# Pacing the first weights by the landing of the x tiles, throwaway matmuls in TensorE's waits, and a last tile in two halves, in an eight-core decoder step

## The chip, the cores and the metric

The kernel runs on all 8 cores of one Trainium2 chip, two dies of four cores. Each core works on its own prompt and its own four samples, and the cores exchange nothing. The metric is the device time of the slowest core in microseconds (us), as a median of several executions.

Such a program has a second, slower state: in some executions one die runs at a lower granted clock (0.812 on four cores in a run of the kernel before that took 2145.57 us). All comparisons here are between fast runs. Where a sentence speaks of "span" it means the time from the first to the last instruction of one core in the trace; the device time is 1.5 to 2.5 us longer. In the views, PE is TensorE's matmuls and PEld its weight loads, DVE is VectorE, ACT ScalarE, POOL GpSimd and SP SyncE; a "q" after a name marks the engine's sequencer, which issues transfers. L80 is the one line of a helper through which every recorded operation goes, so operations are told apart by their tiles.

## The reference

One layer of a hybrid decoder: half an FFN, a mixer of three branches, half an FFN, a final norm. Cut to what matters here:

```python
def rmsnorm(x, g):
    xf = x.astype(jnp.float32)
    y = xf * lax.rsqrt(jnp.mean(xf * xf, axis=-1, keepdims=True) + EPS)
    return (y * g.astype(jnp.float32)).astype(x.dtype)

def half_ffn(x, g, w_gate, w_up, w_down):
    h = rmsnorm(x, g)
    return (jax.nn.silu(h @ w_gate) * (h @ w_up)) @ w_down

# per layer, for prompt (2048 rows a core) and samples (4 rows a core) alike:
x = x + 0.5 * half_ffn(x, *ffn1)
x = x + merge_branches(attention, hgrn2, memory)       # the mixer, cut here
x = x + 0.5 * half_ffn(x, *ffn2)
# at the end:
y = rmsnorm(x, g_final)
```

The model width is 1024 and the FFN's 2816 = 22 x 128. The change touches the first norm and the first gate and up products (the head), and the last down product and the final norm (the tail).

## The kernel before

A core's 2052 rows are six tiles of 352, 336, 336, 352, 336 and 340 columns; a tile of x is `[128, 8, n]` in f32, 1.38 to 1.44 MB. The first half of the program works on tiles 0 to 2, which this document calls the first, second and third tile.

The kernel's Python does not write instructions in the order of the source. It records operations, and a small list scheduler ("the planner") gives every engine one fixed order, using its own table of durations and landing times. On the chip each engine runs that order strictly: an operation whose data is ready still stands behind the one planned before it. PSUM tiles come from pools that hand out banks in order:

```python
# planner
DMA_RATE = {SP: 130.0, POOL: 190.0, ACT: 100.0}          # bytes per ns that it assumes per queue
# ...
def grab(o, t):
    for v in o["allocs"]:
        pl = v.pool
        while pl.first < len(pl.tiles) and pl.tiles[pl.first].unit is not None:
            pl.first += 1                                   # first tile without a bank
        if v.seq > pl.first + pl.ahead:
            return None, pl                                 # too far ahead of it: parked
        # ... take a free bank
# ...
psA = P.pool(bu[0:5], True, 3)                              # gate, up and down products: 5 banks, 3 ahead
```

The head:

```python
def sq(k, c, late=1000.0, pair=True):                       # with pair=False, as in the head
    # ...
    actf(b.t[:, 0:n], xv(k, c), AF.Square, [dx[k][c]], [b.d])
    mm(p.t[:, 0:n], ones_n, b.t[:, 0:n], c == 0, c == 7, [b.d, dc], [p.d], late=late)

def rstd(k):                                                # Ln, then Exp(-0.5 * ..), on ACT
    # ...
    lnexp(r.t[:, 0:n], p.t[:, 0:n], -0.5, [p.d], [r.d])
    return r

def to_h(k, r, g):                                          # the normalized tile, on DVE
    for c in range(8):
        stt(DVE, hT[:, c, t0:t0 + n], xv(k, c), g[:, c:c + 1], r.t[:, 0:n], ALU.mult, ALU.mult, ...)

def gate_up(half, w, hook=None):
    for j in range(NJ):                                     # 22 weights, each 1 MB read as f32, 512 KB as bf16
        b = load_w(..., 2048, first_w[min(j, 5)] if hook else ())   # POOL's queue; waits for these x parts
        for k in HT[half]:                                  # three tiles
            pg, pu = P.tile(psA), P.tile(psA)
            for p, a in ((pg, 0), (pu, 1)):
                for c in range(8):
                    mm(p.t[:, 0:n], wv[:, a, c, :], hT[:, c, t0:t0 + n], c == 0, c == 7, [b.d, dh[k][c]], [p.d])
            actf(s.t[:, 0:n], pg.t[:, 0:n], AF.Silu, [pg.d], [s.d])
            tt(DVE, act[:, j, o:o + n], pu.t[:, 0:n], s.t[:, 0:n], ALU.mult, ...)

first_w = [dx[0][0:4], dx[0], dx[1][0:4], dx[1], dx[2][0:4], dx[2]]
# ...
load_x(0, xt, 4, queues=(SP, ACT))
# ... constants ...
P.dma(ACT, lambda e: e.dma_start(out=vec[:, 0:52], in_=vecs), writes=[dc])
for k in range(3):
    if k:
        load_x(k, xt, 2, after=dx[k - 1][0:5] if k == 1 else dx[k - 1][0:4])
    for c in range(8):
        sq(k, c, 0.0, False)
    to_h(k, rstd(k), gf1)
```

The tail is the general `down`, which does the last two 128-row output chunks tile by tile, and `fin`, which squares, sums, scales and stores a whole tile:

```python
def down(half, w, done):
    def one(k, dp, bs):
        p = P.tile(psA)
        for j in range(NJ):
            mm(p.t[:, 0:n], ..., act[:, j, o:o + n], j == 0, j == NJ - 1, ...)
        stt(DVE, xv(k, dp), p.t[:, 0:n], 0.5, xv(k, dp), ALU.mult, ALU.add, ...)   # residual
        sq(k, dp)
    # ... chunks 0 to 5 for all three tiles, then
    for k in HT[half]:
        for dp, bs in last:                                 # chunks 6 and 7
            one(k, dp, bs)
        done(k)                                             # fin(k): Ln, Exp, eight scalings, four stores
```

The softmax here doesn't subtract the row's maximum and nothing guards it: scores larger than these inputs give would overflow.

## Time and profile before

| what | value | view |
|---|---|---|
| device time, median of 3 runs | 1804.74 us (1804.11 to 1805.31) | times |
| TensorE (PE) busy | 1738.2 us, 96% of the span | the page, part 1 |
| share of PE in the chain that ended last | 90% | the page, part 4 |
| PE idle between 160 and 1730 us | 15.1 us | the waits view |
| gate and up matmuls begun by 50 us | 74 | windows |
| last down matmul to the end of the span | 18.3 us | timeline |

The page of the kernel before has the span, the busy time of each engine (with its share and its number of instructions), and the chain of work that ended last, by engine:

```profile
span 1802.6 us, 33178 instructions; the slowest of 8 cores (1797.5 to 1802.6 us)
...
PE 1738.2 (96%) x12105; PEld 1109.0 (62%) x12171; DVE 674.7 (37%) x1391; ACT 730.4 (41%) x1266; POOL 405.2 (22%) x543
...
PE 90%; DVE 3%; ACT 3%; issue 2%; DMA 1%; POOL 1%; DVEq 0%; ACTq 0%; SPq 0%; POOLq 0%
```

TensorE is nearly always busy, so time can be won only where it is not: at the start and at the end. The windows view of core 2, restricted to the instructions that read or write the normalized tile `hT`, counts gate and up matmuls. Its columns are the stretch and its length, the busy time (and number) of PE, of weight loads and of DVE, the granted TensorE clock, the DMA engines' share and GB/s:

```profile
20.00:30.00 10.00, 3.91 (x16) 1.87 (x16) 4.06 (x8) 1.00 0.99 263
30.00:40.00 10.00, 7.15 (x32) 3.58 (x32) 3.92 (x8) 0.83 1.04 196
40.00:50.00 10.00, 6.42 (x26) 3.48 (x27) 3.92 (x8) 0.66 0.64 143
0.00:50.00 50.00, 17.48 (x74) 8.93 (x75) 11.90 (x24) 0.90 0.83 182
```

At the warm spacing of 0.143 us, 74 matmuls are 10.6 us of work in 50 us, so 39.4 us are lost in the head. The clock falls to 0.83 and 0.66 as well: after the pauses TensorE is cold, that is, it runs at a lower granted clock.

The timeline of core 2 shows why. Its columns are the start, the duration of the group, engine, line, operation, output and input, shape and number; in brackets the idle time of the engine before it and what ended it.

```profile
2.19 0.34 ACTq L80 DMA_DIRECT2D vec<-vecs  x1
...
9.54 3.94 ACT L80 ACTIVATE br<-XA,vec 128x352 bf16<-128x352 f32 x8 [5.98 <-DMA vec<-vecs]
...
14.17 0.56 ACT L80 ACTIVATE fr<-hb,vec 128x352 f32<-128x352 f32 x1 [0.69 <-PE hb L80]
...
21.17 0.57 ACT L80 ACTIVATE br<-XA,vec 128x336 bf16<-128x336 f32 x1 [6.44 <-DMA XA<-xt]
...
21.65 0.57 ACT L80 ACTIVATE fr<-fr,vec 128x352 f32<-128x352 f32 x1
...
22.32 4.06 DVE L80 SCALAR_TENSOR_TENSOR hT<-XA,vec,fr 128x352 bf16<-128x352 f32 x8 [20.59 <-ACT fr L80]
...
23.06 0.79 PE L80 MATMUL ps<-hT,wp 128*128 128x352 bf16 x2
...
42.87 3.92 DVE L80 SCALAR_TENSOR_TENSOR hT<-XA,vec,fr 128x336 bf16<-128x336 f32 x8 [1.93 <-ACT fr L80]
```

The squares of the first tile wait until 9.54 us for the small vector of constants, not for x, though the last part of x had landed only at 9.2. The Ln of the first tile runs at 14.17, but its Exp only at 21.65: it stands in ACT's fixed order behind one square of the second tile (21.17), which waits 6.44 us for its load.

The timeline of core 2 at the end:

```profile
1781.70 2.61 PE L80 MATMUL nd<-actb,wp 128*128 128x340 bf16 x17
...
1783.52 3.91 DVE L80 SCALAR_TENSOR_TENSOR XB<-XB,vec,fr 128x336 f32<-128x336 f32 x8
...
1787.35 0.50 DVE L80 SCALAR_TENSOR_TENSOR XB<-nd,XB 128x340 f32<-128x340 f32 x1
...
1791.56 4.53 DVE L80 SCALAR_TENSOR_TENSOR XB<-XB,vec,fr 128x340 f32<-128x340 f32 x5 [3.71 <-ACT fr L80]
...
1797.36 0.35 ACTq L80 DMA_DIRECT2D yt<-XB  x1
```

The last down matmul ends at 1784.31. Then DVE still scales the tile before (1783.52 for 3.91 us) ahead of the last residual addition.

### The profile page before, as it was taken

The page shows a single profiled execution, that of the slowest core. Times are in us where ns is not written, and L with a number is a line of the kernel's source. Part 1 is how long each engine was busy: PE and PEld are TensorE (multiplying, and loading weights), DVE is VectorE, ACT ScalarE, POOL GpSimd, SP SyncE. Part 2 cuts the span into 40 slices and gives each one's busy share as a digit, 9 for nine tenths or more (in the row PEclk, how much of TensorE's full clock was granted, in tenths as well). Part 3 has the DMA queues.
Part 4 walks back from the last instruction along what each step waited for, and adds up shares of the span by engine and source line. Part 5 has one row for each costly group of instructions (what it writes and reads, how often), then busy time and mean ns, then how long its engine had stood idle before and what let it go on. Part 6 is the DMA issues. An engine that isn't in the chain of part 4 may idle for free.

```text
span 1802.6 us, 33178 instructions; the slowest of 8 cores (1797.5 to 1802.6 us)
## 1 busy us (share of the span) xinstructions
PE 1738.2 (96%) x12105; PEld 1109.0 (62%) x12171; DVE 674.7 (37%) x1391; ACT 730.4 (41%) x1266; POOL 405.2 (22%) x543
## 2 busy tenths in 40 slices
PE   4999999999999999999999999999999999999996
PEld 1666666666655545555556566666666666666663
DVE  2223314222142435756576533543452221422213
ACT  5334414222145566758776633433342221322212
POOL 1112221001244051433431122322220002100021
PEclk9999999999999999999999999999999999999998
DMA  8486459656688554654547745596875447899562
GB/s 196 80 167 127 70 102 197 123 122 127 120 211 199 142 120 77 122 98 93 96 100 152 170 80 88 106 193 130 164 147 87 69 104 145 163 192 171 104 141 96
DMA packets 89391, 234.00 MB, mean 130 GB/s; under 512 B 32912, under 2 KB 40336, under 8 KB 86416
## 3 DMA queue, kind: packets, MB, share of 16 engines
q0 software_dynamic: 40608, 127.03, 44.6%
q1 hardware_dynamic: 46224, 59.26, 10.4%
q10 hardware_dynamic: 2400, 45.57, 8.7%
q8 instruction: 102, 1.67, 0.4%
q14 instruction: 57, 0.47, 0.1%
HBM read 321.27 MB, written 80.51 MB: 223 GB/s over the span
## 4 chain that ended last, share of the span: by engine, by line
PE 90%; DVE 3%; ACT 3%; issue 2%; DMA 1%; POOL 1%; DVEq 0%; ACTq 0%; SPq 0%; POOLq 0%
PE ps L80 49%; PE nd L80 33%; PE hb L80 8%; DVE XB L80 1%; ACT fr L80 1%; DMA XA<-xt 1%; DVE hT L80 1%; DVE br L80 1%; ACT br L80 0%; ACT L80 0%; ACT XA L80 0%; DVE fr L80 0%; POOL XA L80 0%; DVE XA L80 0%; POOL fr L80 0%
## 5 line engine op out<-in xcount | busy, mean ns | idle before, releaser
L80 PE MATMUL ps<-hT,wp 128*128 128x336 bf16 (+4 forms) x3839 | 637.2, 312 | 5.7 <-DVE hT L80 3.8
L80 PEld LDWEIGHTS ps<-hT,wp 128*128 128x128 bf16 x3856 | 365.6, 98 | 208.3 <-issue 6.4
L80 PE MATMUL nd<-hT,wp 128*128 128x336 bf16 (+4 forms) x2547 | 434.5, 312 | 1.4 <-ACT fr L80 0.2
L80 PEld LDWEIGHTS nd<-hT,wp 128*128 128x128 bf16 x2560 | 243.3, 98 | 134.7 <-issue 2.0
L80 ACT ACTIVATE fr<-ps,vec 128x336 f32<-128x336 f32 (+3 forms) x269 | 150.1, 560 | 343.8 <-PE ps L80 343.4
L80 PE MATMUL ps<-actb,wp 128*128 128x336 bf16 (+2 forms) x1612 | 253.8, 308 | 0.3 <-DVE XB L80 0.3
L80 PEld LDWEIGHTS ps<-actb,wp 128*128 128x128 bf16 x1612 | 157.3, 98 | 76.7 <-issue 0.6
L80 ACT ACTIVATE fr<-nd,vec 128x336 f32<-128x336 f32 (+3 forms) x185 | 103.4, 560 | 235.5 <-PE nd L80 235.2
L80 DVE TENSOR_TENSOR actb<-ps,fr 128x336 bf16<-128x336 f32 (+2 forms) x160 | 81.9, 514 | 266.2 <-PE ps L80 260.9
L80 PE MATMUL nd<-actb,wp 128*128 128x336 bf16 (+2 forms) x1076 | 173.0, 308 | 0.7 <-ACT fr L80 0.7
L80 POOL TENSOR_TENSOR fr<-fr 128x512 f32<-128x512 f32 (+3 forms) x96 | 108.0, 1132 | 161.0 <-DVE fr L80 140.2
L80 POOL DMA_DIRECT2D wp<-wgu x88 | 47.4, 538 | 400.3 <-PE ps L80 229.9
L80 PEld LDWEIGHTS nd<-actb,wp 128*128 128x128 bf16 x1076 | 105.0, 98 | 52.3 <-issue 1.0
L80 POOL TENSOR_TENSOR br<-fr 128x336 bf16<-128x336 f32 (+2 forms) x84 | 77.3, 923 | 181.2 <-ACT fr L80 181.0
L80 DVE TENSOR_TENSOR actb<-nd,fr 128x336 bf16<-128x336 f32 (+2 forms) x104 | 53.2, 513 | 173.2 <-PE nd L80 167.2
L80 ACT ACTIVATE fr<-XB,vec 128x352 f32<-128x352 f32 (+2 forms) x96 | 53.9, 577 | 138.5 <-DVE XB L80 138.5
L80 PE MATMUL hb<-hT,wp 128*128 128x512 bf16 (+1 forms) x514 | 95.2, 312 | 1.0 <-ACT fr L80 0.2
L80 ACT ACTIVATE fr<-XA,vec 128x336 f32<-128x336 f32 (+1 forms) x72 | 40.9, 578 | 130.2 <-DVE XA L80 130.2
L80 POOL DMA_DIRECT2D wp<-wd x64 | 34.8, 544 | 249.6 <-PE ps L80 128.5
L80 PE MATMUL hb<-br,cb 128*128 128x336 bf16 (+7 forms) x188 | 48.5, 300 | 28.9 <-ACT br L80 22.9
L80 ACT ACTIVATE fr<-fr,vec 128x512 f32<-128x512 f32 (+3 forms) x105 | 72.6, 700 | 5.0
L80 DVE SCALAR_TENSOR_TENSOR fr<-fr,ps 128x336 f32<-128x336 f32 (+2 forms) x85 | 43.2, 510 | 77.6 <-ACT fr L80 77.6
(244 smaller groups left out, 1630.9 us busy)
## 6 DMA issues: line engine op xcount, KB each, us to landing
wp<-wgu POOLq DMA_DIRECT2D x88, 512.0 KB, 8.9
wp<-wd POOLq DMA_DIRECT2D x64, 352.0 KB, 5.8
wp<-w_gb POOLq DMA_DIRECT2D x48, 384.0 KB, 8.8
wp<-w_hqf POOLq DMA_DIRECT2D x16, 512.0 KB, 8.3
vd<-br SPq DMA_DIRECT2D x48, 128.0 KB, 4.0
XA<-vd SPq DMA_DIRECT2D x12, 512.0 KB, 5.7
wp<-w_qk POOLq DMA_DIRECT2D x12, 512.0 KB, 7.6
pv<-fr SPq DMA_DIRECT2D x21, 256.0 KB, 6.4
```

Source lines behind the costliest of these rows:

```text
L80: return f(*[g(x) for x in a], **{n: g(x) for n, x in k.items()})
```

## The change

In the head, all x tiles are queued at once in four parts each, the constants first; the first weight goes at once, later ones when given parts of x have landed; squares go to ACT or DVE; and the planner puts throwaway matmuls wherever it plans a wait of TensorE in the first 60 us. It also assumes 150 bytes per ns on every queue in the first 30 us. In the tail, the last tile is done as two halves of 168 and 172 columns, each with its own sum, scaling and store; outputs are written into a contiguous buffer; Exp also writes its result to PSUM, from where DVE's scalings read it; two or three of the eight scalings go to ACT and POOL. The core of the diff, cut:

```diff
+    HEAD = 30000.0
+    HEAD_RATE = 150.0
+    fill, fill_end, FILL = None, 0.0, 65.0
 # planner
+            if e == PE and order[PE] and self.fill is not None and start < self.fill_end:
+                o["fill"] = max(0, int((start - free[e] - 150.0) / self.FILL))
-                    pipe[e] = max(pipe[e], start + issue) + o["nbytes"] / self.DMA_RATE[e]
+                    t = max(pipe[e], start + issue)
+                    pipe[e] = t + o["nbytes"] / (self.HEAD_RATE if t < self.HEAD else self.DMA_RATE[e])
 # emission
+                        for _ in range(o.get("fill", 0)):
+                            self.fill(e)
+    psA2 = P.pool(bu[0:4], True, 3)
+    psS2 = P.pool(bu[4:8], True, 0)
+    psS0 = P.pool(bu[5:7], True, 0)
+    def sq_first(k, c):
+        p, b, x = pss[k], P.tile(brp), xv(k, c)
+        P.op((ACT, DVE), (... AF.Square ..., ... tensor_tensor x * x ...), reads=[dx[k][c], dc], writes=[b.d])
+        mm(p.t[:, 0:n], ones_n, b.t[:, 0:n], c == 0, c == 7, [b.d, dc], [p.d])
-    first_w = [dx[0][0:4], dx[0], dx[1][0:4], dx[1], dx[2][0:4], dx[2]]
+    first_w = [(), dx[0][0:6], dx[1][0:6], dx[2][0:4]]
-    load_x(0, xt, 4, queues=(SP, ACT))
+    P.dma(ACT, lambda e: e.dma_start(out=vec[:, 0:52], in_=vecs), writes=[dc])
+    for k in range(3):
+        load_x(k, xt, 4)
+    P.fill = lambda e: e.matmul(bu[7].t[:, 0:128], lhsT=ones_n, rhs=ones_n, start=True, stop=True)
+    P.fill_end = 60e3
     for k in range(3):
-        if k:
-            load_x(k, xt, 2, after=dx[k - 1][0:5] if k == 1 else dx[k - 1][0:4])
         for c in range(8):
-            sq(k, c, 0.0, False)
+            sq_first(k, c)
         to_h(k, rstd(k), gf1)
 # ... four memsets of POOL moved later ...
+    def down_last(w):
+        parts = [(3, 0, FT[3][1]), (4, 0, FT[4][1]), (5, 0, 168), (5, 168, FT[5][1] - 168)]
 # ... chunks 0 to 4 for (0,), (1,), (2, 3); chunks 5 to 7 part by part ...
+        def root(pi):
+            actf(r.t[:, 0:n], p.t[:, 0:n], AF.Ln, [p.d, dc], [r.d], bias=epsc)
+            actf(p.t[:, 0:n], r.t[:, 0:n], AF.Exp, [r.d], [p.d], scale=-0.5)
+            actf(r.t[:, 0:n], r.t[:, 0:n], AF.Exp, [r.d], [r.d], scale=-0.5)
+        def scale(pi, r):
+            ov = xv(k, 0, 8) if pi < 2 else XA[:, 8 * u:8 * (u + n)]
+                    if c in ((1, 3, 5) if pi < 2 else (1, 3)):
+                        actf(x, x, AF.Identity, [d], [d], scale=gfi[:, c:c + 1])
+                        tt(POOL, y, x, r.t[:, 0:n], ALU.mult, [d, r.d], [od[c]])
+                    else:
+                        stt(DVE, y, x, gfi[:, c:c + 1], ps2[pi].t[:, 0:n], ALU.mult, ALU.mult, ...)
-    down(1, wdn[1], fin)
+    down_last(wdn[1])
```

The host puts the two halves of the last tile together when it assembles the outputs.

More of the change, by code (lines that the diff above doesn't have):

```diff
@@ L722, in sq @@
             mm(p.t[:, 0:n], ones_n, b.t[:, 0:n], c == 1, c == 7, [b.d, dc], [p.d], late=late)
+    def sq_first(k, c):
+        n = FT[k][1]
+        if c == 0:
+            pss[k] = P.tile(psS0)
+        p, b, x = pss[k], P.tile(brp), xv(k, c)
+        P.op((ACT, DVE), (lambda e: e.activation(out=b.t[:, 0:n], in_=x, func=AF.Square, bias=zeroc, scale=1.0),
+                          lambda e: e.tensor_tensor(out=b.t[:, 0:n], in0=x, in1=x, op=ALU.mult)), reads=[dx[k][c], dc], writes=[b.d])
+        mm(p.t[:, 0:n], ones_n, b.t[:, 0:n], c == 0, c == 7, [b.d, dc], [p.d])
     def rstd(k):
@@ L745, in gate_up @@
         for j in range(NJ):
-            b = load_w(w[j].rearrange("p a c n -> p (a c n)"), 2048, first_w[min(j, 5)] if hook else ())
+            b = load_w(w[j].rearrange("p a c n -> p (a c n)"), 2048, first_w[min(j, 3)] if hook else ())
             wv = b.t[:, :].rearrange("p (a c n) -> p a c n", a=2, c=8)
@@ L1359, in bulk_at @@
         return 1760e3
-    load_x(0, xt, 4, queues=(SP, ACT))
-    P.op(POOL, lambda e: e.memset(vec[:, 60:61], 1.0), writes=[d_one])
+    P.dma(ACT, lambda e: e.dma_start(out=vec[:, 0:52], in_=vecs), writes=[dc])
+    for k in range(3):
+        load_x(k, xt, 4)
+    P.op(DVE, lambda e: e.memset(vec[:, 60:61], 1.0), writes=[d_one])
     P.op(ACT, lambda e: e.activation(out=vec[:, 63:64], in_=vec[:, 60:61], func=AF.Ln), reads=[d_one], writes=[d_one])
@@ L1367, in build_nc @@
     P.op(DVE, lambda e: e.memset(vec[:, 62:63], 0.0), writes=[dc])
-    P.dma(ACT, lambda e: e.dma_start(out=vec[:, 0:52], in_=vecs), writes=[dc])
+    P.op(PE, lambda e: e.matmul(bu[7].t[:, 0:128], lhsT=ones_n, rhs=ones_n, start=True, stop=True), reads=[dc])
+    P.fill = lambda e: e.matmul(bu[7].t[:, 0:128], lhsT=ones_n, rhs=ones_n, start=True, stop=True)
+    P.fill_end = 60e3
     for k in range(3):
-        if k:
-            load_x(k, xt, 2, after=dx[k - 1][0:5] if k == 1 else dx[k - 1][0:4])
         for c in range(8):
-            sq(k, c, 0.0, False)
+            sq_first(k, c)
         to_h(k, rstd(k), gf1)
-    P.op(POOL, lambda e: e.memset(ones_b, 1.0), writes=[dm])
-    P.op(POOL, lambda e: e.memset(ones_h, 1.0 / 128), writes=[dm])
-    P.op(POOL, lambda e: e.memset(rst, 1.0), writes=[dm])
-    P.op(POOL, lambda e: e.memset(cb[:, 896:1408:64], 0.0), writes=[dm])
     for q, (src_, dst_) in enumerate(bulk):
@@ L1386, in hook @@
         elif j == 5:
+            P.op(POOL, lambda e: e.memset(ones_b, 1.0), writes=[dm])
+            P.op(POOL, lambda e: e.memset(ones_h, 1.0 / 128), writes=[dm])
+            P.op(POOL, lambda e: e.memset(rst, 1.0), writes=[dm])
+            P.op(POOL, lambda e: e.memset(cb[:, 896:1408:64], 0.0), writes=[dm])
             P.dma(ACT, lambda e: e.dma_start(out=cf[:, :], in_=cstf), reads=d_memT, writes=[dm])
@@ L1503, in fin @@
             for c in (2 * q, 2 * q + 1):
-                eng = POOL if k == 5 and c in (1, 4, 7) else DVE
-                if eng == DVE:
-                    stt(DVE, xv(k, c), xv(k, c), gfi[:, c:c + 1], r.t[:, 0:n], ALU.mult, ALU.mult, [dx[k][c], r.d, dc], [dx[k][c]])
-                else:
-                    tt(POOL, xv(k, c), xv(k, c), r.t[:, 0:n], ALU.mult, [dx[k][c], r.d], [dx[k][c]])
-                    actf(xv(k, c), xv(k, c), AF.Identity, [dx[k][c]], [dx[k][c]], scale=gfi[:, c:c + 1])
@@ L1510, in fin @@
-            src, dst = xv(k, 2 * q, 2), yt[k][:, 2 * q * n:(2 * q + 2) * n]
-            P.dma((SP, ACT)[q % 2] if k == 5 else SP, lambda e, src=src, dst=dst: e.dma_start(out=dst, in_=src), reads=dx[k][2 * q:2 * q + 2])
+                stt(DVE, xv(k, c), xv(k, c), gfi[:, c:c + 1], r.t[:, 0:n], ALU.mult, ALU.mult, [dx[k][c], r.d, dc], [dx[k][c]])
+            src, dst = xv(k, 2 * q, 2), yt[k][:, 2 * q * n:(2 * q + 2) * n]
+            P.dma(SP, lambda e, src=src, dst=dst: e.dma_start(out=dst, in_=src), reads=dx[k][2 * q:2 * q + 2])
@@ new lines, in down_last, with xdep, mmsum, one @@
+    def down_last(w):
+        parts = [(3, 0, FT[3][1]), (4, 0, FT[4][1]), (5, 0, 168), (5, 168, FT[5][1] - 168)]
+        ps2 = [P.tile(psS2) for _ in parts]
+        dxs = {2: [Dep() for _ in range(8)], 3: [Dep() for _ in range(8)]}
+        dy = {2: [Dep() for _ in range(8)], 3: [Dep() for _ in range(8)]}
+        yl = (yt[3], yt[4], yt[5][:, 0:8 * 168], yt[5][:, 8 * 168:])
+        def xdep(pi, c):
+            return dxs[pi][c] if pi in dxs else dx[parts[pi][0]][c]
+        def mmsum(pi, b, lo, first, last):
+            _, u, n = parts[pi]
+            mm(ps2[pi].t[:, 0:n], ones_n, b.t[:, lo:lo + n], first, last, [b.d, dc], [ps2[pi].d], late=1000.0)
+        def one(pis, dp, bs):
+            k, u0 = parts[pis[0]][0:2]
+            n = sum(parts[pi][2] for pi in pis)
+            o = FT[k][0] - 1024 + u0
+            p = P.tile(psA2)
+            for j in range(NJ):
+                b = bs[j // 11]
+                mm(p.t[:, 0:n], b.t[:, (j % 11) * 128:(j % 11 + 1) * 128], act[:, j, o:o + n], j == 0, j == NJ - 1, [b.d, dact[1][k % 3]], [p.d])
+            x = xv(k, dp)[:, u0:u0 + n]
+            d = dx[k][dp] if dp < 5 else xdep(pis[0], dp)
+            stt(DVE, x, p.t[:, 0:n], 0.5, x, ALU.mult, ALU.add, [p.d, d], [d])
+            if pis[0] == 3 and dp > 4:
+                b = P.tile(brp)
+                actf(b.t[:, 0:n], x, AF.Square, [d], [b.d])
+                mmsum(3, b, 0, False, dp == 7)
+            elif dp == 4 or (pis[0] == 2 and dp == 5):
+                b = P.tile(brp)
+                actf(b.t[:, 0:n], x, AF.Square, [d], [b.d])
+                for pi in pis:
+                    mmsum(pi, b, parts[pi][1] - u0, False, False)
+            elif dp in (0, 2, 5, 6) and not (pis[0] < 2 and dp == 6):
+                pss[k, 0] = P.tile(frp)
+                actf(pss[k, 0].t[:, 0:n], x, AF.Square, [d], [pss[k, 0].d])
+            elif pis[0] < 2 and dp == 6:
+                s, s2 = pss[k, 0], P.tile(frp)
+                actf(s2.t[:, 0:n], x, AF.Square, [d], [s2.d])
+                tt(POOL, s.t[:, 0:n], s.t[:, 0:n], s2.t[:, 0:n], ALU.add, [s.d, s2.d], [s.d])
+            else:
+                b, s, s2 = P.tile(brp), pss[k, 0], P.tile(frp)
+                actf(s2.t[:, 0:n], x, AF.Square, [d], [s2.d])
+                tt(POOL, b.t[:, 0:n], s.t[:, 0:n], s2.t[:, 0:n], ALU.add, [s.d, s2.d], [b.d])
+                for pi in pis:
+                    mmsum(pi, b, parts[pi][1] - u0, dp == 1, dp == 7)
+        def root(pi):
+            n = parts[pi][2]
+            r, p = P.tile(frp), ps2[pi]
+            actf(r.t[:, 0:n], p.t[:, 0:n], AF.Ln, [p.d, dc], [r.d], bias=epsc)
+            actf(p.t[:, 0:n], r.t[:, 0:n], AF.Exp, [r.d], [p.d], scale=-0.5)
+            actf(r.t[:, 0:n], r.t[:, 0:n], AF.Exp, [r.d], [r.d], scale=-0.5)
+            return r
+        def scale(pi, r):
+            k, u, n = parts[pi]
+            ov = xv(k, 0, 8) if pi < 2 else XA[:, 8 * u:8 * (u + n)]
+            od = dx[k] if pi < 2 else dy[pi]
+            for q in range(4):
+                for c in (2 * q, 2 * q + 1):
+                    x, y = xv(k, c)[:, u:u + n], ov[:, c * n:(c + 1) * n]
+                    d = xdep(pi, c)
+                    if c in ((1, 3, 5) if pi < 2 else (1, 3)):
+                        actf(x, x, AF.Identity, [d], [d], scale=gfi[:, c:c + 1])
+                        tt(POOL, y, x, r.t[:, 0:n], ALU.mult, [d, r.d], [od[c]])
+                    else:
+                        stt(DVE, y, x, gfi[:, c:c + 1], ps2[pi].t[:, 0:n], ALU.mult, ALU.mult, [d, ps2[pi].d, dc], [od[c]])
+                if q % 2:
+                    o, w = (2 * q - 2) * n, 4 * n
+                    src, dst = ov[:, o:o + w], yl[pi][:, o:o + w]
+                    P.dma((SP, ACT)[q // 2] if pi == 3 else SP, lambda e, src=src, dst=dst: e.dma_start(out=dst, in_=src), reads=[od[c] for c in range(2 * q - 2, 2 * q + 2)])
+        def ld(dp):
+            return [load_w(w[dp, jh].rearrange("p j n -> p (j n)"), 1408) for jh in range(2)]
+        P.op(ACT, lambda e: e.activation(out=vec[:, 63:64], in_=vec[:, 60:61], func=AF.Ln), reads=[d_one, dact[1][2]], writes=[d_one])
+        for dp in range(5):
+            bs = ld(dp)
+            for pis in ((0,), (1,), (2, 3)):
+                one(pis, dp, bs)
+        for pi in dxs:
+            switch(dxs[pi], dx[5])
+            switch(dy[pi], dx[0])
+        tails = [(dp, ld(dp)) for dp in (5, 6, 7)]
+        rs = []
+        for pi in range(4):
+            for dp, bs in tails:
+                one((pi,), dp, bs)
+            rs.append(root(pi))
+            if pi == 2:
+                scale(0, rs[0])
+        for pi in (1, 2, 3):
+            scale(pi, rs[pi])
@@ L1605, in _assemble @@
     cat = lambda k: np.stack([np.asarray(R[i][k], dtype=np.float32) for i in range(nc_)], axis=0)
-    y = np.concatenate([cat(f"yt{k}").reshape(nc_, 128, 8, n) for k, (t0, n) in enumerate(FT)], axis=3).transpose(0, 3, 2, 1).reshape(nc_, NT, D)
+    yp = [cat(f"yt{k}") for k in range(6)]
+    yp[5:] = [yp[5][:, :, 0:8 * 168], yp[5][:, :, 8 * 168:]]
+    y = np.concatenate([a.reshape(nc_, 128, 8, -1) for a in yp], axis=3).transpose(0, 3, 2, 1).reshape(nc_, NT, D)
     outs = [y[:, 0:T], y[:, T:NT].reshape(4 * nc_, 1, D)]
```

## The prediction

> **What bounds the kernel now.** TensorE. The page shows PE busy 1738 of 1802.6 us; the chain of waits is 90% PE. The waits view shows only some 15 us of PE idling between 160 and 1740 us. Gains can come only from the two ends.
>
> *Head (windows, timeline).* Up to 50 us PE ran 98 matmuls, 24 of them sums of squares, so 74 gate/up matmuls. At the warm spacing of 0.143 us that is 10.7 us of work: 39 us are lost. Reasons: the first square waits for the vector constants, queued behind x parts, until 9.5 us. About 20 us of the chain are waits for x tiles: the second is issued at 9 us, after the first lands, and shares the DMA engines with two 1 MB weight reads (DMA share 0.86 to 0.97 from 10 to 20 us); its halves land at 21.1 and 24.0 us. The first tile's Exp stands in ACT's queue behind a square of the second tile and runs at 21.65 us, though its Ln ran at 14.2. After each pause PE runs cold: 336-column matmuls are 0.28 us apart (granted clock 0.56 to 0.76 between 40 and 50 us). The Trainium skill ("TensorE: Matmul & The Clock Gate", What's actually happening) gives half clock until about 3.4 us of activity; this trace agrees, a few us per pause.
>
> *Tail (timeline).* The last down matmul ends at about 1784.3 us, the span at 1802.6: 18.3 us. In it DVE scales the tile before (3.9 us) ahead of the last residual addition (1787.35), then square, add, sum, Ln, Exp, eight scalings, the last store issued at 1797.36, landing 2.7 us later.
>
> **What the change does.**
> - Head: all x parts are queued at once, constants first, squares on ACT and DVE; the first weight goes at once, later ones by landings. This removes idle queue time, not bytes. x plus three weights are about 7.3 MB; this trace read roughly 330 GB/s between 9 and 32 us, so I estimate landings near 12, 19 and 27 us. The first tile may land 3 us later than now (9.05), since all queues share the same engines (skill, "DMA: Bandwidth & Descriptors", Issuing engines are not separate DMA queues). First gate matmul near 14.5 us (now 23.0), PE continuous from 25 to 30 us.
> - Throwaway matmuls keep PE warm. 128-column matmuls are about 57 ns apart in the attention part (four in 0.39 us), so they should fit; too many would delay real work by 1 to 2 us.
> - Head loss falls from 39 to about 20 us: 19 us gained.
> - Tail: halves of 168 and 172 columns. At 57 ns for 128 columns with their own weights, 168 should cost 72: no PE penalty. After the last matmul: residual 0.35, square 0.45, add 0.5, sum 0.35, Ln and Exp 0.85, six DVE scalings 2.1, hand-overs 1, store 2.7, end 2: about 11 us. 7 us gained.
> - The middle is rescheduled, a few us either way.
>
> **Predicted: 1779 us, 1770 to 1789.** Faster by over 2% (under 1768.6) 0.07, within 2% 0.92, slower 0.01.
>
> **Right if:** x tiles land by 13, 20 and 28 us, granted clock near 1.0 from 15 us, 170 to 210 gate/up matmuls done by 50 us, last down matmul to the end 10 to 12 us, middle stalls near 15 us.
> **Wrong if:** contention delays the first tile past 15 us, throwaway matmuls overrun, table switches on ACT still stall PE, POOL adds or scalings stand ahead of the last half tile's chain, or the new order stalls the middle.

## The result, and the profile after

The change takes 1789.53 us in the median (four runs, 1788.77 to 1790.00), beside 1804.88 for the kernel before (four runs). The ratio is 0.9915, with a 95% interval of 0.9898 to 0.9932: within 2%, as predicted, but half a microsecond above the predicted range, and 10.5 us above the predicted 1779. Ratios in this document are the mean time of one kernel's fast runs over that of the other's of the same rounds, so they are not quite the ratio of the medians quoted.

The page of the change, span and busy times:

```profile
span 1786.5 us, 34018 instructions; the slowest of 8 cores (1786.0 to 1786.7 us)
...
PE 1753.3 (98%) x12527; PEld 1127.3 (63%) x12527; DVE 677.7 (38%) x1408; ACT 733.4 (41%) x1271; POOL 406.8 (23%) x548
```

The windows view of core 5 of the change, again of `hT` alone:

```profile
20.00:30.00 10.00, 3.04 (x17) 1.17 (x17) 3.30 (x8) 1.00 0.79 176
30.00:40.00 10.00, 6.36 (x42) 3.89 (x41) 5.11 (x12) 1.00 0.99 195
40.00:50.00 10.00, 10.00 (x72) 6.78 (x70) 0.95 (x2) 1.00 1.04 175
0.00:50.00 50.00, 21.11 (x134) 12.36 (x135) 11.90 (x24) 1.00 0.91 193
```

The clock is 1.00 throughout, as hoped, and TensorE is full from 40 us. But by 50 us it has done 134 gate and up matmuls, not 170 to 210. At 0.143 us each, the head still loses 30.8 us. The timeline of core 5:

```profile
1.56 0.71 POOL L80 DMA_DIRECT2D wp<-wgu  x1 [0.85 <-POOLq L560]
...
13.37 1.07 ACT L80 ACTIVATE br<-XA,vec 128x352 bf16<-128x352 f32 x2 [4.88 <-DMA XA<-xt]
...
14.05 1.50 PE L1391 MATMUL hb<-cb 128*128 128x128 bf16 x24
...
17.45 4.05 DVE L80 SCALAR_TENSOR_TENSOR hT<-XA,vec,fr 128x352 bf16<-128x352 f32 x8 [2.04 <-ACT fr L80]
...
18.18 0.46 PE L80 MATMUL ps<-hT,wp 128*128 128x352 bf16 x2 [0.37 <-DVE hT L80]
...
21.42 0.92 DVE L80 TENSOR_TENSOR br<-XA 128x336 bf16<-128x336 f32 x2
...
22.04 1.28 ACT L80 ACT_TABLE_LOAD   x1 [3.76 <-PE ps L80]
...
23.79 1.03 ACT L80 ACTIVATE br<-XA,vec 128x336 bf16<-128x336 f32 x2
...
25.34 1.28 ACT L80 ACT_TABLE_LOAD   x1 [0.53 <-PE hb L80]
26.64 0.54 ACT L80 ACTIVATE fr<-hb,vec 128x336 f32<-128x336 f32 x1
...
28.21 3.92 DVE L80 SCALAR_TENSOR_TENSOR hT<-XA,vec,fr 128x336 bf16<-128x336 f32 x8 [2.78 <-ACT fr L80]
...
34.20 3.46 PE L1391 MATMUL hb<-cb 128*128 128x128 bf16 x59
...
37.02 3.92 DVE L80 SCALAR_TENSOR_TENSOR hT<-XA,vec,fr 128x336 bf16<-128x336 f32 x8 [1.61 <-ACT fr L80]
```

Line 1391 is the throwaway matmul. The last parts of the three tiles land at 13.3, 17.4 and 28.3 us, close to the estimates of 12, 19 and 27. Their normalized forms come at 17.45, 28.21 and 37.02 us. So the second tile is in memory at 17.4 but usable only from 28.2. Its squares are late already: two run on DVE behind the scaling of the first tile (21.42), and the last two on ACT behind the Silu of the first product (23.79). From 22.1 to 28.9 and from 34.2 to 37.7 TensorE runs next to nothing but sums and throwaway matmuls: 59 of those from 34.20 alone.

The timeline of core 5 at the end:

```profile
1770.46 4.10 PE L80 MATMUL ps<-actb,wp 128*128 128x172 bf16 x53
...
1774.84 0.83 PE L80 MATMUL ps<-actb,wp 128*128 128x172 bf16 x9
...
1776.07 0.33 DVE L80 SCALAR_TENSOR_TENSOR XB<-ps,XB 128x172 f32<-128x172 f32 x1
...
1778.41 1.91 DVE L80 SCALAR_TENSOR_TENSOR XA<-XB,vec,nd 128x172 f32<-128x172 f32 x6 [0.52 <-ACT nd L80]
...
1780.41 0.36 ACTq L80 DMA_DIRECT2D yt<-XA  x1
```

The last down matmul ends at 1775.67 and the span at 1786.7, 11.0 us later, where the prediction said 11. The 53 matmuls of 172 columns take 4.10 us; with 0.24 us for one alone, that is (4.10 - 0.24) / 52 = 74 ns from one to the next.

To divide the gain I use one mark: the moment POOL issues the 23rd FFN weight, which is the first of the down products. It is issued as a buffer comes free, so it follows TensorE's progress through gate and up.

| | before | change |
|---|---|---|
| mark, mean of 8 cores | 157.1 us | 150.1 us |
| mark, earliest and latest core | 154.4 to 159.3 | 149.6 to 150.4 |
| from mark to last down matmul, slowest core | 1625.0 | 1625.3 |
| last down matmul to end of span, slowest core | 18.3 | 11.0 |

The slowest core wins 8.9 us in the head, of 19 predicted, and about 7 in the tail, of 7 predicted. The middle and the halves cost nothing: the PE part from mark to last down matmul is equal within 0.3 us, and PE's idle time between 160 and 1730 us is 13.4 us (15.1 before). So the question for the experiments is the head: where did the other 10 us go?

The mark in the timelines of POOL, first on core 2 before, then on core 5 of the change:

```profile
159.28 0.57 POOL L80 DMA_DIRECT2D wp<-wd  x1 [4.09 <-PE ps L80]
```

```profile
150.36 0.57 POOL L80 DMA_DIRECT2D wp<-wd  x1 [4.10 <-PE ps L80]
```

The latest core of a program sets its time. Before, the cores' spans (1797.5 to 1802.6 us) follow their marks (154.37 on core 6, 159.28 on core 2), and the marks follow the landing of the second tile. On core 6 its first half lands at 14.8 us, on core 2 at 21.1. ACT on core 6:

```profile
14.88 0.58 ACT L80 ACTIVATE br<-XA,vec 128x336 bf16<-128x336 f32 x1 [1.03 <-DMA XA<-xt]
...
15.36 0.58 ACT L80 ACTIVATE fr<-fr,vec 128x352 f32<-128x352 f32 x1
```

So the first tile's Exp, behind that square, runs at 15.36 us and not at 21.65, and the first gate matmul at 16.78 and not at 23.06. Over all eight cores: where the half tile lands by 14.8 to 17.6 us (cores 0, 3, 4 and 6) the mark is at 154.4 to 155.9, where it lands at 20.3 to 21.1 (cores 1, 2, 5 and 7) at 157.9 to 159.3. The cold time does not order the cores: the mean granted clock from 20 to 50 us is 0.83 on seven of them and 0.89 on core 5. This is read from the traces and not tested by an edit. In each of the pairs 0 and 1, 2 and 3, 4 and 5, 6 and 7 one core gets its half tile 3.3 us or more before the other; why is not shown. In the change the first tile's Exp waits for no other tile's load, and the spread of the spans is 0.7 us instead of 5.1; e2 below, cold but in the same order, has 2.2. As the spread shrinks, the slowest core wins 8.9 us and the mean core 7.0.

### The profile page after: what moved, and what is told of

Its sections match the earlier page's. It is cut to its first block, busy times and chain, and to the rows that moved or that the text cites. A ratio compares the mean times of both kernels' runs of the same rounds, so it can differ in the third digit from the quotient of the medians.

```text
span 1786.5 us, 34018 instructions; the slowest of 8 cores (1786.0 to 1786.7 us)
## 1 busy us (share of the span) xinstructions
PE 1753.3 (98%) x12527; PEld 1127.3 (63%) x12527; DVE 677.7 (38%) x1408; ACT 733.4 (41%) x1271; POOL 406.8 (23%) x548
## 4 chain that ended last, share of the span: by engine, by line
PE 92%; DVE 2%; ACT 2%; issue 2%; DMA 1%; POOL 0%; DVEq 0%; SPq 0%; ACTq 0%; POOLq 0%
PE ps L80 51%; PE nd L80 32%; PE hb L80 8%; ACT fr L80 1%; DVE hT L80 1%; DVE br L80 1%; DMA XA<-xt 1%; DVE XB L80 0%; ACT br L80 0%; ACT L80 0%; PE hb L1391 0%; DVE XA L80 0%; ACT XA L80 0%; DVE fr L80 0%; POOL XA L80 0%
## 5 line engine op out<-in xcount | busy, mean ns | idle before, releaser
L80 PE MATMUL ps<-actb,wp 128*128 128x336 bf16 (+4 forms) x1782 | 271.5, 304 | 1.0 <-ACT fr L80 0.7
L80 PEld LDWEIGHTS ps<-actb,wp 128*128 128x128 bf16 x1782 | 171.3, 98 | 80.7 <-issue 1.7
L80 ACT ACTIVATE fr<-nd,vec 128x336 f32<-128x336 f32 (+4 forms) x184 | 103.3, 562 | 228.3 <-PE nd L80 227.8
L80 PE MATMUL nd<-actb,wp 128*128 128x336 bf16 (+3 forms) x972 | 154.3, 307 | 0.2 <-ACT fr L80 0.2
L80 PEld LDWEIGHTS nd<-actb,wp 128*128 128x128 bf16 x972 | 94.4, 98 | 45.5 <-issue 0.6
L80 POOL TENSOR_TENSOR br<-fr 128x336 bf16<-128x336 f32 (+3 forms) x81 | 73.8, 913 | 155.7 <-ACT fr L80 155.5
L80 ACT ACTIVATE fr<-XB,vec 128x352 f32<-128x352 f32 (+3 forms) x92 | 51.5, 576 | 116.2 <-DVE XB L80 116.2
L80 ACT ACTIVATE fr<-fr,vec 128x512 f32<-128x512 f32 (+4 forms) x106 | 73.2, 698 | 5.5 <-ACT fr L80 0.4
L80 PE MATMUL hb<-hT,wp 128*128 128x512 bf16 (+1 forms) x400 | 74.9, 319 | 0.2 <-DVE XB L80 0.2
L80 PE MATMUL ps<-wp,hT 128*128 128x512 bf16 x224 | 54.5, 379 | 1.6 <-DVE hT L80 1.6
## 6 DMA issues: line engine op xcount, KB each, us to landing
wp<-wgu POOLq DMA_DIRECT2D x88, 512.0 KB, 10.5
```

The lines of the kernel that those rows point to most:

```text
L80: return f(*[g(x) for x in a], **{n: g(x) for n, x in k.items()})
```

## The experiments

The leading theory is that the data was there and the fixed order held it back: bank hand-out, ACT's order with its table switches, and a plan made for other landing times. The rivals are that throwaway matmuls overrun real work, and that the landings themselves (shared DMA engines) hold the head. Where a recorded expectation names theories by letter, the words beside the letter say what it expects of that run. Fifteen kernels ran. Those of one group shared a chip and the runs of the kernel before: e1 to e4, e5 to e8, e9 to e12, e13 to e15. The fast runs of the kernel before have means from 1804.8 to 1808.5 us in the groups, with its spread of cores, while the change had medians of 1789.53 and 1789.17 in the two groups where it ran; so I compare times of the new kernels across groups with some care, and lean on the mark.

### Do the two ends add up? e1_tail_only and e6_head_only, with e5_change_again

Edit of e1: the kernel before with `down_last` and its outputs, nothing of the head. Edit of e6: the change with `down(1, wdn[1], fin)` and the old `fin` in place of `down_last`. e5 is the change, unaltered.

```diff
 # e1: the head of before, with
-    down(1, wdn[1], fin)
+    down_last(wdn[1])
 # e6: the head of the change, with
-    down_last(wdn[1])
+    down(1, wdn[1], fin)
```

> The old head with the new tail (the last tile in two halves). The order before the last down stage is that of the kernel before. If the tail gave what the two traces show (18.3 us from the last down matmul to the end before, about 11.2 after), this run is 6.5 to 7.5 us faster than before, about 1797.5 us. If the tail's gain was less and the head's more, it is nearer 1801.

> The change itself, unedited, on the chip of the runs beside it, as the mark to compare them with: 0.9915 of before, core spans within 1 us of each other near 1786.4 us.

> The new head with the old tail (one tile, one chain, five DVE and three POOL scalings). If head and tail add up, this run is 7 us slower than the change (the tail's 18.3 us instead of 11.2) and about 8.5 us faster than before, near 1796.5. If the head gives less than half of the whole gain, it is above 1799.

Measured: e1 took 1801.31 us (median of its three fast runs; ratio 0.9967, 0.9951 to 0.9984), with the mark at 157.1 us as in the kernel before. Of 6.5 to 7.5 us expected it gives 5.9: its tail takes 11.05 us on every core, but from the mark to the last down matmul its slowest core takes 1629.8 us and not 1625, with a wait of 2.4 us for one of the later weights (w_gb) among the causes. e6 took 1794.64 us (two fast runs; ratio 0.9935, 0.9914 to 0.9957), with the mark at 150.1 as in the change. e5 took 1789.17 us (ratio 0.9905). In means of fast runs the tail alone gives 5.9 us (on another chip), the head alone 11.6, both 17.0. So the parts add up within a microsecond and neither spoils the other. The head's 11.6 is larger than the 8.9 of the first comparison in part because on this chip the kernel before took 1.4 us longer (1806.2 in the mean of fast runs, beside 1804.8); the rest is not explained.

### Do the throwaway matmuls help or hold? e2_no_fill and e11_fewer_throwaways

```diff
 # e2
-    P.fill = lambda e: e.matmul(bu[7].t[:, 0:128], lhsT=ones_n, rhs=ones_n, start=True, stop=True)
 # e11: one throwaway for every 100 ns of planned wait, not every 65
-    fill, fill_end, FILL = None, 0.0, 65.0
+    fill, fill_end, FILL = None, 0.0, 100.0
```

> The change without its throwaway matmuls; order and waits of all real work unchanged. Theory A (PE is kept from ready work by the order in which PSUM banks are handed out; the throwaway matmuls cost nothing and keep the clock up): slower than the change by 2 to 5 us, because each of the three bursts of gate/up work starts at half clock; first gate matmul not before 17 us, gate/up matmuls up to 50 us fewer than 134. Rival B (the throwaway matmuls overrun and push real work back): first gate matmul 1 to 3 us earlier than 18.15 us and the whole 1 to 3 us faster than the change.

> The change with about 60% of its throwaway matmuls (178 of 282), orders unchanged. If too many of them push the first sums back by about 0.8 us, as the run without any suggests, while the clock stays up with fewer: first normalised value at 16.7 to 17.0 us instead of 17.45, clock still 1.0 in the bursts, 0.5 to 1 us faster than the change. If the clock falls between bursts: 1 to 3 us slower.

Measured, e2: 1791.88 us in the mean of two fast runs (two more were slow). The mark comes 3.2 us later, at 153.3. The granted clock between 20 and 50 us is 0.80 to 0.85 instead of 1.00, and 107 matmuls instead of 134 are done by 50 us. The first gate matmul, though, starts at 17.41 us, 0.77 earlier. So the throwaways do cost the first tile about 0.8 us, and pay 3.2 net by keeping the clock. The Trainium skill ("TensorE: Matmul & The Clock Gate", What's actually happening) says that the clock is halved until about 3.4 us of activity, judged in a free-running window; this agrees on the halving: a gate matmul takes 0.28 us from one to the next cold and 0.143 warm. The stretch can be longer than 3.4 us: in e2, gate matmuls that begin at 28.47 us stay cold until about 33.9.

Measured, e11: 1790.13 us (ratio 0.9898), no faster. I expected half to one microsecond. On the slowest core the first normalized tile comes 0.9 us earlier (16.52), but the clock sags to 0.97 in the head and the third comes at 38.44 instead of 37.02; the mark is 149.9 in the mean and 151.8 there. The other seven cores of this trace stay at 1.00, with marks of 149.1 to 150.0. So one core that goes cold sets the time, and fewer throwaways (178 in the trace instead of 282) move the mean mark by only 0.2 us.

### Do the banks hold it? e3_banks_ahead

In the change's plan, gate and up tiles may take a bank only if they are at most three ahead of the first tile without one. The order is weight 0 on tiles one, two, three, then weight 1 on tile one. Each of these takes two banks. So the product of weight 1 with the first tile, in memory from 23.7 and 13.3 us, cannot get banks until weight 0 has met the second tile, from 28.9 us. The edit lets the planner look 12 ahead, for the first tiles of this pool only:

```diff
+    wide = None
-                if v.seq > pl.first + pl.ahead:
+                if v.seq > pl.first + (12 if pl is self.wide and pl.first < 12 else pl.ahead):
     psA = P.pool(bu[0:5], True, 3)
+    P.wide = psA
```

> The change, with the PSUM bank pool letting ready tiles go up to 12 places ahead (3 now) as long as its first 12 tiles are not placed; nothing else edited. Theory A: the second weight's matmuls on the first x tile run in the hole between 22 and 29 us, and more in the hole between 34 and 38 us; gate/up matmuls up to 50 us rise from 134 to 165 to 175 and the time falls by 4 to 6 us, to about 1784.5. Rivals B (throwaway matmuls) and C (table switches and the order on ACT delay the x tiles' normalisation): the holes stay, within 1 us of the change.

Measured: 1785.34 and 1786.59 us in its two fast runs (two more were slow; 1785.96 / 1807.54 = 0.9881), with the mark at 146.4 us, 3.7 earlier than in the change. The gain in time is there. The count of matmuls by 50 us is 150 on the slowest core and 161 in the mean, below the 165 to 175 that I expected. The timeline of TensorE on the slowest core shows one reason:

```profile
23.16 0.73 PE L80 MATMUL ps<-hT,wp 128*128 128x352 bf16 x2 [1.78 <-DMA wp<-wgu]
```

Weight 1 now meets the first tile, but it lands only near 23 us, and TensorE waits 1.78 us for it. On this core alone the clock also falls to 0.83 between 20 and 30 us. The new plan has fewer throwaways as well, 198 instead of 282; e11 shows that this by itself moves the mean mark by only 0.2 us. So the bank order was one cause.

### Do ACT's table switches hold it? e4_no_table_switch, and e9_both_limits_off

In the change, ACT runs the Silu of the first product at about 23 us, between two table loads of 1.28 us (22.04 and 25.34), ahead of the second tile's Ln at 26.64. The edit replaces Silu with Identity for the first three weights, so that no switch is needed. The output is wrong (relative error 0.078). e9 is this with the edit of e3.

```diff
-                actf(s.t[:, 0:n], pg.t[:, 0:n], AF.Silu, [pg.d], [s.d])
+                actf(s.t[:, 0:n], pg.t[:, 0:n], AF.Identity if hook and j < 3 else AF.Silu, [pg.d], [s.d])
```

> The change, with Identity in place of Silu for the first three weights (wrong results on purpose), so that ACT needs no table load between the Ln and Exp of the three x tiles. Rival C (table switches and ACT's order hold up the second and third x tile): the third tile's normalised values come 2 to 4 us earlier than 37.0 us, gate/up matmuls up to 50 us rise from 134 by 15 to 25 and the time falls by 2 to 4 us. Theory A alone: the holes are set by bank order and landings, less than 1 us.

> Bank order opened and Identity in place of Silu for the first three weights (wrong results on purpose), the two single edits together. The mark is the issue of the 23rd FFN weight, which the change reached at 150.1 us as a mean of the cores, bank order alone at 146.4 and no table switch alone at 146.7. If the two are separate limits: 143 to 144.5 us here, the time about 1782.5. If they are one and the same wait seen from two sides: 146 us, no better than either. The estimate of the prediction (39 us lost falling to 20) would need about 138.

Measured, e4: 1785.86 us (mean of fast runs; ratio 0.9880, 0.9865 to 0.9895), mark 146.7, that is 3.4 earlier. The normalized second and third tiles come at 24.88 and 33.26 us, and 160 matmuls are done by 50 us. So the switches were a cause too: each stands in the one chain that makes the next tile usable. The 3.4 us include what the planner does with the edit, for it counts no switch either and orders ACT, DVE and TensorE anew (233 throwaways instead of 282).

Measured, e9: 1782.87 us (ratio 0.9859), mark 144.4, as expected (143 to 144.5). Together the two edits give 5.7 us, less than 3.7 + 3.4 = 7.1: partly they remove the same wait.

### Do the landings hold it? e7_no_pacing, e10_first_weight_later, e15_third_weight_later

```diff
-    first_w = [(), dx[0][0:6], dx[1][0:6], dx[2][0:4]]
 # e7: no weight waits for x
+    first_w = [(), (), (), ()]
 # e10: the first weight waits for half of the first tile
+    first_w = [dx[0][0:4], dx[0][0:6], dx[1][0:6], dx[2][0:4]]
 # e15: the third weight waits for half of the third tile
+    first_w = [(), dx[0][0:6], dx[2][0:4], dx[2][0:4]]
```

> The change with no weight waiting for an x tile: all seven weight buffers are filled at once. The planned order of every engine is the same as in the change, so only the landings differ. If the pacing matters because all queues share the DMA engines: the first tile lands 4 to 10 us later than 13.4 us, first gate/up matmul at 22 to 28 us instead of 18.15, and the run is 4 to 10 us slower than the change. Rival (landings are not what holds the head; the bank order and ACT are): within 1.5 us.

> The change with the first weight held until half of the first x tile has landed, as it was before; orders stay the planned ones. If the unpaced first weight is what moved the landing of the first x tile from 9 to 13.4 us: the tile lands at 10.5 to 11.5 us, but the first weight itself only at 16 to 18 us, first gate/up matmul within 1.5 us of 18.15 and the time within 1.5 us of the change. If the tile still lands after 12.5 us, the later x tiles in the same queue are the cause.

> The change with the third weight held until half of the third x tile has landed; planned orders are the same. If the third weight's sharing moves the third x tile: it lands by 24 to 25 us instead of 28.2, but as the orders and the throwaway matmuls are those planned for 31 us, the mark moves by less than 1 us (149.5 to 150.5), or later if the third weight is then late. If landings are what holds the change: the mark 2 to 3 us earlier.

Measured, e7: 1803.42 us in two fast runs, 14.2 more than e5 of the same rounds and nearly the time of the kernel before (ratio 0.9984, 0.9963 to 1.0006). I expected 4 to 10. The timeline of e7:

```profile
1.56 3.36 POOL L80 DMA_DIRECT2D wp<-wgu  x6 [0.86 <-POOLq L560]
...
16.69 1.07 ACT L80 ACTIVATE br<-XA,vec 128x352 bf16<-128x352 f32 x2 [8.81 <-DMA XA<-xt]
...
22.65 0.46 PE L80 MATMUL ps<-hT,wp 128*128 128x352 bf16 x2
```

Six weights are issued at once. From 6 to 34 us the weights' queue takes 60 to 76% of the DMA time and x only 24 to 35%; the first tile lands at 16.6 us instead of 13.3, the three normalized tiles come at 21.92, 40.18 and 51.57, and 48 matmuls are done by 50 us. This agrees with the Trainium skill ("DMA: Bandwidth & Descriptors", Issuing engines are not separate DMA queues): issuing weights and x from different engines does not keep them apart. Pacing weights by the landing of x is worth 14 us against none, with every engine's order and the throwaways left as planned for the paced landings; a plan fitted to the unpaced ones was not run, so part of the 14 us may be the plan's. The kernel before paced them as well, by other parts of x.

Measured, e10: 1789.41 us (ratio 0.9895), no change, although the first tile now lands at 9.8 us, 3.5 earlier. The timeline of e10, ACT and TensorE:

```profile
9.89 1.07 ACT L80 ACTIVATE br<-XA,vec 128x352 bf16<-128x352 f32 x2 [2.43 <-DMA XA<-xt]
...
13.60 1.50 PE L1391 MATMUL hb<-cb 128*128 128x128 bf16 x24
...
15.67 0.56 ACT L80 ACTIVATE fr<-hb,vec 128x352 f32<-128x352 f32 x1 [4.71 <-PE hb L80]
```

The squares are done early, but the sums on TensorE stand behind batches of 24 throwaways, which the planner put there for the landing that it had assumed. ACT waits 4.71 us for the sums. The normalized first tile gains 0.45 us (17.00), and the mark stays at 150.1. But the edit trades one wait for another: the first weight now lands at 17.6 to 19.6 us over the cores (11.0 to 12.2 in the change), and the planner, which knows that it comes later, puts a batch of 23 throwaways before the first gate matmul, where the change has 3. This starts at 18.46 us on the slowest core and at 18.9 in the mean, beside 17.9 in the change. So e10 does not test an earlier first tile alone.

Measured, e15: 1789.41 us (ratio 0.9893). The third tile lands at 25.9 us instead of 28.3, a little later than the 24 to 25 expected; its normalized form comes at 36.86 (37.02) and the mark stays at 150.0. Here the orders and throwaways are those of the change. So in the change as it is, an earlier landing of the third tile is worth nothing; for the first tile e10 leaves it open. Much later landings, as in e7, hurt at once.

### Does a better plan recover it? e8_ahead_faster_plan, e12_plan_by_landings, e13_exp_before_square, e14_and_no_table_switch

The planner's own table, printed on the host, gives head times close to the real ones: it plans the second normalized tile at 26.96 us, and with the 1.07 us until the first load is issued that is 28.03, beside 28.21 measured; for the third 37.4 beside 37.0. It assumes landings of 22.1 and 31.3 us for the second and third tile, where the trace has 17.4 and 28.3. Four edits change what it assumes. e8 is e3 with a faster rate; e12 is e3 with rates by time, fitted to the landings seen; e13 is e12 with the squares of the third tile made to wait for the second tile's Exp; e14 is e13 with the Identity of e4. Its output is wrong, which doesn't matter for the time.

```diff
 # e8, with the edit of e3
-    HEAD_RATE = 150.0
+    HEAD_RATE = 200.0
 # e12, with the edit of e3
-                    pipe[e] = t + o["nbytes"] / (self.HEAD_RATE if t < self.HEAD else self.DMA_RATE[e])
+                    r = (110.0 if t < 22e3 else 190.0) if e == POOL else 150.0 if t < 8e3 else 240.0 if t < 14.3e3 else 120.0
+                    pipe[e] = t + o["nbytes"] / (r if t < self.HEAD else self.DMA_RATE[e])
 # e13, with the edits of e12 (in sq_first and the head loop)
-... reads=[dx[k][c], dc], writes=[b.d])
+... reads=[dx[k][c], dc] + ([rs1[k - 1].d] if k == 2 else []), writes=[b.d])
-        to_h(k, rstd(k), gf1)
+        rs1[k] = rstd(k)
+        to_h(k, rs1[k], gf1)
```

> Bank order opened as in the earlier run, and the planner's rate for the first loads raised from 150 to 200 bytes per ns, so that ACT, DVE and PE are ordered for x tiles that land earlier, as they do (the second by 18 us, planned for 22). If the wrong plan costs the second tile several us: its normalised values start at 23 to 25 us instead of 28.2, gate/up matmuls up to 50 us reach 170 to 185, and the run is 6 to 9 us faster than the change, about 1781. If engines then stand waiting in a wrong order (for the second weight, landing at 23 us), the gain over the earlier run with bank order alone is under 1 us.

> Bank order opened, and the planner's rates set piecewise to what the trace of the change showed (first x tile until 13 us, second until 17.7, third until 29, first weights about 11 us each). Ordering by true landings: the second tile's normalised values at 25.5 to 26.5 us instead of 28.2, gate/up matmuls up to 50 us about 165 to 180, the mark (23rd weight) at 144 to 145 us, against 146.4 with bank order alone. If planning is not the limit: 146 or later.

> As the plan by landings, and the squares of the third x tile may not start before the second tile's Exp, so the Exp no longer stands behind a square that waits for a load until 27.6 us. If that order costs what it seems to: Exp at 25.9 instead of 28.07 us, the second tile's normalised values at 26.6 instead of 28.7, the mark (23rd weight) at 142 to 143 us instead of 144.1, the time 1 to 2 us less. If the third tile's landing limits: the hole moves to before the third tile and the mark stays within 0.7 us of 144.1.

> The same, with Identity in place of Silu for the first three weights (wrong results on purpose). Table loads on ACT stand between the second tile's sums and its Ln (1.3 us) and before the third's (1.3 us). If they still cost: the mark 1 to 2.5 us before the run beside it. If landings of x and the weights now limit: under 0.7 us.

Measured, e8: 1789.62 us (ratio 0.9908), a miss. Now the plan is wrong the other way: it orders weights' matmuls earlier than the weights land. On the slowest core TensorE waits 2.66 us for the second weight (until 22.63), and the second tile's Ln runs at 29.71, behind two Silus of that work. Most spans lie near 1783.5 or near 1787, and the mark between 146.4 and 151.3. The clock is a second cause: with 126 throwaways instead of 282 it falls to between 0.66 and 0.83 on every core from 20 to 30 us. I did not separate the two. A plan that is too hopeful gives back part of what the banks gave.

Measured, e12: 1783.31 us (ratio 0.9862, 0.9845 to 0.9879), correct, mark 144.1, 167 matmuls by 50 us. That is 6 us of the missing 10.8 with no change of the real work and no wrong output; the throwaways fall to 162, which e11 shows to matter little by itself. The timeline of ACT in e12, on its slowest core, shows the order striking once more:

```profile
24.02 1.28 ACT L80 ACT_TABLE_LOAD   x1
25.31 0.54 ACT L80 ACTIVATE fr<-hb,vec 128x336 f32<-128x336 f32 x1
...
27.59 0.58 ACT L80 ACTIVATE br<-XA,vec 128x336 bf16<-128x336 f32 x1 [1.74 <-DMA XA<-xt]
...
28.07 0.56 ACT L80 ACTIVATE fr<-fr,vec 128x336 f32<-128x336 f32 x1
```

The second tile's Ln runs at 25.31, its Exp at 28.07, behind a square of the third tile that waits for its load: just what the kernel before did with the first and second tile. On cores 0, 6 and 7 that part of x lands in time, and the Exp follows its Ln after 0.9 us.

Measured, e13: 1782.77 us (ratio 0.9856, 0.9840 to 0.9873), correct, the best version that ran: 6.8 us under the change's 1789.53. On the slowest core the normalized second tile comes 1.9 us earlier (26.88), in the mean of the cores 0.95; 173 matmuls are done by 50 us there, but in the mean 177 as in e12, and the mark stays at 144.1. Against e12 the gain is 0.8 us in the mean of fast runs, on another chip; since the mark did not move, I do not count it as shown.

Measured, e14: 1782.04 us in the mean of three fast runs, a fourth being slow (ratio 0.9853), mark 143.5. Once the order fits, taking the table switches away is worth 0.6 us, not 3.4.

## Why the prediction was right or wrong

What was right:

- The bound. TensorE is the limit, and gains came only from the two ends; the middle did not move (1625.0 and 1625.3 us from mark to last down matmul).
- The landings: 13.3, 17.4 and 28.3 us, beside 12, 19 and 27.
- The clock: 1.00 in the head, and e2 shows that the throwaway matmuls do it (3.2 us net).
- The tail: 11.0 us after the last matmul, beside "about 11", and no penalty from halves (74 ns for 172 columns, beside an estimate of 72 for 168). e1 shows 5.9 us for the tail alone, with a slower middle on its slowest core.
- The verdict, within 2%.

What was wrong is one term of the sum: "Head loss falls from 39 to about 20 us: 19 us gained", with its ground "PE continuous from 25 to 30 us". The measured loss is 30.8 us; TensorE is continuous only from 37.7 us. That the head loses to late starts and to cold pauses was right; the term was mis-sized by 10.8 us:

- 3.7 us, because the first gate matmul starts at 18.18 and not near 14.5. Set against my sum, the landing is 1.3 us later and the throwaways are in the way for 0.8 (e2); the rest, about 1.6, is a longer chain of sum, Ln, Exp and scaling than I allowed: 2.5 us from landing to first gate matmul, where e2, without throwaways, takes 3.9 (13.5 to 17.41). This is an account and not a test: e10 moved the landing by 3.5 us, but then the throwaways hold the sums and the first weight comes late.
- About 6 us, because work that was ready did not run. This is shown: with the same transfers, a wider bank hand-out and a plan fitted to the landings, e12 moves the mark by 6.0 us and the time to 1783.31. Against the rival that its fewer throwaways did it speaks e11 (0.2 us). The bank order alone is worth 3.7 (e3), the table switches alone 3.4 (e4), both 5.7 (e9).
- About 1 us stays open.

The step that failed is thus the one from "the tiles land at 12, 19 and 27" to "PE continuous from 25 to 30". It took TensorE to use a tile as soon as it lands. In this kernel the second tile lands at 17.4 us and becomes usable at 28.2, because its squares stand behind the first tile's scaling and the Silu of the first product, and its Ln behind a second table load; meanwhile the next weight's product with the tile already there has no bank. My list of what could be wrong named table switches and throwaways; it gave them no size, and it did not name the bank order or the planner's assumed landings at all. The evidence could have been read before: the kernel before shows a finished Ln (14.17) whose Exp waits until 21.65 behind another tile's square.

What stays open: from e13's mark of 144.1 us to what my term would have needed, about 138 (the mark before on the slowest core, 159.3, less 19, is 140; for the mean core, 157.1 less 19, it is 138), some 4 to 6 us. The first gate matmul near 18 us and the landing of the third tile both lie there; I did not separate them. Nor did I run e10's earlier landing together with fewer throwaways, which might shorten the first tile's chain.

## What to carry to other kernels

A landing time is not a start time: between them lies the in-order chain on the small engines, and with a fixed order whatever was planned ahead of it counts, including table loads, a square of the next tile, and a bank that is not handed out yet. When loads are moved, give the scheduler the landings that the trace shows, on neither side (e8 and e12), and look at how far its buffers may be given out of order. On many cores the slowest one is the time, so look at their spread too; and pacing weight loads behind the activations that everything waits for was worth 14 us here, against no pacing under the same plan.

## What the Trainium skill lacked or had wrong

- "TensorE: Matmul & The Clock Gate", Seeing it yourself: it says to budget 13/16 of the clock for sustained dense matmuls on all cores. Here the fast runs hold a mean granted clock of 0.991 to 0.998 on all eight cores for 1.8 ms; means near 0.81 appear only in slow runs (0.812 on one die in the run of 2145.57 us). The page speaks of the default power profile; which one these chips had is not known.
- "TensorE: Matmul & The Clock Gate", Back-to-back issue gap: it gives about 81 ns for each 128-column matmul with its own weight load. Here 24 throwaway matmuls of 128 columns take 1.50 us, at most 63 ns each, and the 172-column ones follow each other at 74 ns.
- No page gives how far apart the same load lands on the eight cores of one program: before, the first half of the second tile lands between 14.8 and 21.1 us, and the spans differ by 5.1 us (1797.5 to 1802.6).
- "ScalarE: Activation LUTs", What ACT_TABLE_LOAD costs: about 2.7 us for a switch including the drain. Here the load takes 1.28 us and the next Ln begins 1.29 us after its start (24.02 and 25.31 in e12). No wait for a drain shows on either side: in the change a load begins at 34.41, 0.02 us after the end of the Silu before it, and the Ln after it at 35.71.
- "DMA: Bandwidth & Descriptors", Queues, rings and completion order: it tells of a round robin by packets, but not what shares come out. Here six weight loads against x gave the weights 60 to 76% of the DMA time and x 24 to 35%, and not pacing them, under the same plan, cost 14.2 us (e7).
